# Dividing a pair of heads' outputs instead of the softmax weights, with casts and lo parts given to other engines

## The chip, the cores and the metric

The kernel runs on one core of a Trainium2 chip. A core has five engines with a queue each, and every engine works through its own queue in order: TensorE (PE in the profile; its weight loads are PEld), VectorE (DVE), ScalarE (ACT), GpSimd (POOL) and SyncE (SP), which here issues DMAs. The metric is the device time of one execution in microseconds (us), lower is better.

## What is computed

A two-layer encoder on 512 tokens of width 1024. Each layer normalises its input, projects it, runs four kinds of attention with four heads of 64 columns each, projects their concatenation back, and then runs a gated feed-forward block. Cut to what matters here:

```python
def one_block(args):                                   # b: differential attention
    s = einsum('bqhcd,bkhcd->bchqk', q_blk, k) * scale + bias
    p = jax.nn.softmax(s, axis=-1)
    a = p[:, 0] - lam * p[:, 1]
    return einsum('bhqk,bkhd->bqhd', a, v)             # then rms_norm(o, subln_g) * (1 - lam_init)
...
    out = jnp.sum(jnp.stack(outs) * wts, axis=0)       # c: dilated, three patterns merged by their sums
...
    p = jax.nn.softmax(s * scale, axis=-1)             # d: latent attention
    return einsum('bhqk,bkhd->bqhd', p, v)
...
mix = jnp.concatenate([o_a, o_b, o_c, o_d], axis=-1)   # o_a: 2D neighborhood attention
x = x + mix @ w_o[l]
h = rms_norm(x, ffn_norm[l])
x = x + (silu(h @ w_gate[l]) * (h @ w_up[l])) @ w_down[l]
```

All of it is in float32.

## The kernel before

Activations lie transposed: 128 features on the partitions, 512 tokens along the free dimension, eight such tiles for the width. TensorE multiplies in a rounded float32 format (fp32r in the profile), so each operand is split into a hi part, a cast of the value to that format, and a lo part, the value minus hi. A product is then three matmuls, hi by hi (L173), hi by lo (L175) and lo by hi (L178). The helper `split` does this for activations, with `copy` (L137 on ScalarE, L139 on VectorE or GpSimd) and `minus` (L142); `slab` does it for a slab of 1024 weight columns that came by DMA: a cast (L137 or L139) and a lo part (L160), which GpSimd makes in two halves of 512 columns and VectorE in one. `whi` and `wlo` have two buffers each. Which engine makes what stands in the table ENG by a tag ('P' GpSimd, 'V' VectorE, 'A' ScalarE); a tag that isn't in it goes to the default of its helper: ScalarE for casts, VectorE for the lo parts of activations, GpSimd for those of attention's weights. A tag holds for both layers.

An attention stage handles the four kinds in the order b, c, d, a (numbers 1, 2, 3, 0 in the code). For b, c and d a unit is one head and one block of 128 queries against all 512 keys; sixteen units each, by pair of heads p, head hh of the pair and block qb. For a there are eight larger units. A unit has three steps. S_ makes the scores in PSUM, `soft` (L676 to L688) adds the bias and takes the row's extreme `mx` on VectorE (L684; for d a plain reduction, L681), exponentiates on ScalarE with the row's sum `den` as a second output (L686) and takes its reciprocal `rd` on VectorE (L687), and `normalise` (L690 to L696) multiplies the 128x512 weights `e` by `rd`, on ScalarE (L692), GpSimd (L694) or VectorE (L696). For b, `s_b` does this with two score tiles: GpSimd multiplies the second by its `rd` and the negated lambda (L755), and VectorE adds the first times its own `rd` (L756). T_ transposes `e` on TensorE, four times 128x128 (L826), and splits the result into `th` (from PSUM, a cast) and `tl` (PSUM minus `th`, always VectorE). V_ multiplies with the values, and after a head's last block `fold` (L759 to L772) adds the two halves of PSUM; after the pair's second head `plain_fin` (c, d) splits the pair's output into a `mix` tile. `b_fin` first takes the root mean square of the rows: squares, column sums on TensorE, a power on GpSimd, and `spread_rows`, which copies the 128x8 result over 128x512 and transposes it so that it lies along the tokens (`obw`).

A loop of steps sets the order (`step`): S_ of the unit three ahead (LEAD), filler work (projections of later stages, output projections), V_ of the unit before, T_ of this one, filler again. The amounts of filler are written out by hand (RATES). The framework then schedules with a simulated time line and puts in all waits; buffers are recycled by tag: tag `ob` has one buffer, the small 128x1 tiles eight.

The feed-forward stage (from L1062) is a plain stream of matmuls over slabs of weights and isn't touched.

Of the kernel before, what the change touches and what calls it, by code (L numbers as in the profile page):

```python
# [42 lines left out]
RAW = 4  # L43
PRE = 0
NQF = 6
ENG = {'m10_l': 'P', 'wh_cq0': 'P', 'rk2': 'V', 'wh_ud1': 'V', 'ea03': 'A', 'wl_kc1': 'V', 'b11_l': 'P', 'fo100': 'V', 'kh_c01': 'V', 'kl_c00': 'P', 'ea13': 'A', 'sc_qn1': 'P', 'kl_d00': 'P', 'fa010': 'P', 'wl_wo04': 'V', 'wh_qb1': 'V', 'ql_d10': 'P', 'kd_d11': 'P', 'm11_h': 'V', 'kd_d01': 'P', 'ed03': 'A', 'wh_kb0': 'V', 'ql_a01': 'P', 'x22': 'P', 'wl_qa1': 'V', 'wh_qb0': 'V', 'ed11': 'P', 'kh_d11': 'V', 'wl_ka0': 'V', 'kl_a10': 'P', 'x27': 'P', 'ec11': 'A', 'wh_vcb': 'V', 'x05': 'P', 'ed13': 'A', 'sc_ka0': 'P', 't301_h': 'V', 'x03': 'P', 'fo010': 'V', 'wh_wo14': 'P', 'kd_d10': 'P', 'wl_wo16': 'V', 'wl_wo14': 'V', 'fa110': 'P', 'fo211': 'V', 'sc_ka1': 'P', 'x15': 'P', 'kl_a11': 'P', 'kd_a01': 'V', 'wh_wo00': 'P', 'wh_ckv': 'V', 'ed02': 'P', 'm30_l': 'P', 'wh_ur': 'V', 'wl_kb1': 'V', 'kh_a10': 'V', 'kl_d10': 'P', 'kd_a11': 'P', 'kh_a11': 'V', 'kd_d00': 'P', 'fo200': 'V', 'ed00': 'P', 'x23': 'P', 'm21_l': 'P', 'kh_d10': 'P', 'ea10': 'A', 'kl_a00': 'P', 'qh_a01': 'P', 'b10_l': 'P', 'fa300': 'P', 'm20_h': 'P', 'kh_c00': 'V', 't203_h': 'V', 'fo310': 'V', 'wl_wo12': 'V', 'x02': 'P', 't210_h': 'V', 'kd_a00': 'P', 'kl_c01': 'P', 'wl_qb1': 'V', 'ec13': 'A', 'rq1': 'V', 'wl_vbb': 'V', 't011_h': 'V', 't100_h': 'V', 'ea00': 'V', 't212_h': 'V', 'qh_c00': 'V', 'kh_c11': 'P', 'kh_d00': 'V', 'fa210': 'P'}
QS = 'ss'
WARM = 12
NV = 2
# [13 lines left out]
def tile_encoder(ctx, tc, xT, gains, lamv, w_in, w_kr, w_d, w_o0, w_o1, w_o2, w_gu, w_dn,  # L63
# [268 lines left out]
    def attention(l, xsrc, x, hs, ssq, pl, nar):  # L332
# [440 lines left out]

        def plain_fin(m):
            def fin(p, hh, pv):
                of = fold(m, p, hh, pv)
                if hh:
                    mt = mix_tile(m, p)
                    split(mt[:, 0, :], mt[:, 1, :], of, f"m{m}{p}")
                    ready.add((m, p))  # L780
            return fin

        def b_fin(p, hh, pv):
            of = fold(1, p, hh, pv)
# [6 lines left out]
            def sums():  # L791
# [73 lines left out]
        def grid_unit(p, hh, b2, need):  # L865
# [4 lines left out]
            def S_():  # L870
# [3 lines left out]
                for bb in range(2):  # L874
# [417 lines left out]
```

## Time and profile before

| | us |
|---|---|
| median of 3 runs (lowest to highest) | 1323.04 (1323.0 to 1323.88) |
| profiled execution | 1322.35 |
| its span, first to last instruction | 1320.5 |
| TensorE busy in the span | 1277.9 |
| VectorE busy | 770.0 |
| ScalarE busy | 563.5 |
| GpSimd busy | 457.2 |

The first attention stage takes about the first 298 us, the first feed-forward stage lasts to about 660, the second attention stage to about 945, and the second feed-forward stage to the end. Busy times over the whole span mix these stages; TensorE's busy time holds the modelled end of each matmul. The profile's words for engines are those of the first section; L142 is line 142 of the kernel; "idle before" is the time in which an engine did nothing ahead of an instruction, and the name behind it is what ended that.

### The profile page before, as it was taken

How to read it: one execution, taken by the hardware profiler on the slowest of the kernel's cores; microseconds unless marked ns; L12 is line 12 of the kernel's file. 1: busy time of each engine (PE TensorE's matmuls, PEld its weight loads, DVE VectorE, ACT ScalarE, POOL GpSimd, SP SyncE). 2: the span in 40 equal slices, each digit the busy share in tenths (PEclk: the TensorE clock that was granted, in tenths of full speed). 3: DMA queues.
4: the chain of work that ended last, by engine and by line, in shares of the span. 5: the costliest groups of instructions: out<-in, count | busy, mean ns of one | idle time of the engine just before them, and what ended most of it. 6: DMA issues, size and time to landing. Idle time of an engine off the chain costs nothing. (4 is left out here: it accounts for less than half of the span.)

```text
span 1320.5 us, 17193 instructions
## 1 busy us (share of the span) xinstructions
PE 1277.9 (97%) x6330; PEld 1066.6 (81%) x6330; DVE 770.0 (58%) x1315; ACT 563.5 (43%) x972; POOL 457.2 (35%) x377
## 2 busy tenths in 40 slices
PE   8999999989999999999999989999899999999997
PEld 7777788867888888888898777788688888888886
DVE  6589989866444444333237989887754444443232
ACT  5456666744333333222225666666533333332230
POOL 1267765544111111100145577454621111111000
PEclk9999999999999999999999999999999999999999
DMA  5652432122222223333345424321132222223321
GB/s 189 183 154 75 138 105 81 50 79 80 96 96 97 98 100 97 99 113 111 111 137 161 121 77 129 98 81 65 64 100 100 101 99 96 96 92 90 99 88 64
DMA packets 50916, 135.63 MB, mean 103 GB/s; under 512 B 7896, under 2 KB 12760, under 8 KB 50832
## 3 DMA queue, kind: packets, MB, share of 16 engines
q1 hardware_dynamic: 50544, 134.25, 32.3%
q8 instruction: 50, 0.82, 0.3%
q10 hardware_dynamic: 288, 0.29, 0.1%
q14 instruction: 34, 0.28, 0.1%
HBM read 119.01 MB, written 4.23 MB: 93 GB/s over the span
## 5 line engine op out<-in xcount | busy, mean ns | idle before, releaser
L175 PE MATMUL gu<-h_f,whi_gu 128*128 128x512 f32 x704 | 274.3, 390 | 1.5 <-DVE h_f L201 1.4
L173 PE MATMUL gu<-h_f,whi_gu 128*128 128x512 f32 x704 | 273.9, 390 | 0.1
L1081 POOL TENSOR_TENSOR u<-u,th 128x512 f32<-128x512 f32 x44 | 93.2, 2118 | 367.6 <-DVE u L1079 351.5
L178 PE MATMUL gu<-h_f,wlo_gu 128*128 128x512 f32 x704 | 173.9, 389 | 0.0
L175 PEld LDWEIGHTS gu<-h_f,whi_gu 128*128 128x128 f32 x704 | 132.0, 188 | 31.0 <-DVE h_f L201 4.0
L173 PEld LDWEIGHTS gu<-h_f,whi_gu 128*128 128x128 f32 x704 | 132.2, 188 | 28.2 <-DVE x L663 0.9
L178 PEld LDWEIGHTS gu<-h_f,wlo_gu 128*128 128x128 f32 x704 | 132.2, 188 | 27.4
L137 ACT CAST whi_gu<-raw_gu 128x1024 fp32r<-128x1024 f32 x88 | 92.7, 1054 | 105.3 <-PE gu L175 104.9
L173 PE MATMUL dn<-act,whi_dn 128*128 128x512 f32 x330 | 128.4, 389 | 0.0
L175 PE MATMUL dn<-act,whi_dn 128*128 128x512 f32 x330 | 128.4, 389 | 0.0
L160 DVE TENSOR_TENSOR wlo_gu<-raw_gu,whi_gu 128x1024 fp32r<-128x1024 f32 x88 | 111.3, 1264 | 19.4 <-ACT whi_gu L137 17.8
L686 ACT ACTIVATE e<-e,mx 128x512 f32<-128x512 f32 (+1 forms) x128 | 85.5, 669 | 73.0 <-DVE mx L684 70.9
L160 DVE TENSOR_TENSOR wlo_dn<-raw_dn,whi_dn 128x1024 fp32r<-128x1024 f32 (+1 forms) x45 | 51.0, 1134 | 100.3 <-PE dn L178 60.9
L1079 DVE SCALAR_TENSOR_TENSOR u<-gu,bc_ff 128x512 f32<-128x512 f32 x44 | 30.4, 691 | 122.8 <-PE gu L178 122.8
L137 ACT CAST whi_dn<-raw_dn 128x1024 fp32r<-128x1024 f32 (+1 forms) x45 | 44.2, 982 | 127.8 <-PE dn L175 111.3
L137 ACT CAST act<-u 128x512 fp32r<-128x512 f32 x44 | 27.3, 621 | 155.1 <-POOL u L1081 155.1
L178 PE MATMUL dn<-act,wlo_dn 128*128 128x512 f32 x330 | 82.1, 389 | 0.0
L142 DVE TENSOR_TENSOR tl<-tp,th 128x512 fp32r<-128x512 f32 x112 | 74.5, 683 | 10.3 <-ACT th L137 9.6
L684 DVE CUSTOM_DVE_ANT_0 e<-sc,t 128x512 f32<-128x512 f32 x96 | 65.1, 684 | 21.3 <-PE sc L751 8.8
L142 DVE TENSOR_TENSOR act<-u,act 128x512 fp32r<-128x512 f32 x44 | 32.7, 743 | 73.6 <-ACT act L137 73.3
L178 PEld LDWEIGHTS dn<-act,wlo_dn 128*128 128x128 f32 x330 | 62.0, 188 | 12.8
L173 PEld LDWEIGHTS dn<-act,whi_dn 128*128 128x128 f32 x330 | 62.0, 188 | 12.8
(433 smaller groups left out, 2719.4 us busy)
## 6 DMA issues: line engine op xcount, KB each, us to landing
raw_gu<-in_w_gu_dram SPq DMA_DIRECT2D x88, 512.0 KB, 3.2
raw_dn<-in_w_dn_dram SPq DMA_DIRECT2D x32, 512.0 KB, 3.5
raw_wo<-in_w_o_dram SPq DMA_DIRECT2D x16, 512.0 KB, 3.9
t<-tb SPq DMA_DIRECT2D x16, 448.0 KB, 3.9
raw_dn<-in_w_dn_dram SPq DMA_DIRECT2D x16, 384.0 KB, 3.1
sb<-kbn SPq DMA_DIRECT2D x64, 64.0 KB, 2.0
sb<-qbn SPq DMA_DIRECT2D x64, 64.0 KB, 2.1
xin<-in_xT_dram SPq DMA_DIRECT2D x8, 256.0 KB, 5.2
```

Of the source, the lines that this page charges most:

```text
L137: nc.scalar.copy(out, src)
L142: engine(tag, usual).tensor_tensor(out, src, hi.bitcast(F32), op=ALU.subtract)
L160: lo_eng.tensor_tensor(lo[:, c], raw[:, c], hi[:, c].bitcast(F32), op=ALU.subtract)
L173: nc.tensor.matmul(pt, whi[:, k, wcol], xs[k][:, 0, :], start=first and k == 0, stop=False)
L175: nc.tensor.matmul(pt, whi[:, k, wcol], xs[k][:, 1, :], start=False, stop=False)
L178: nc.tensor.matmul(pt, wlo[:, k, wcol], xs[k][:, 0, :], start=False, stop=last and k == nk - 1)
L684: nc.vector.tensor_tensor_reduce(out=e, in0=sc, in1=bias, scale=1.0, scalar=BIG, op0=ALU.add, op1=ALU.min, accum_out=mx)
L686: nc.scalar.activation(e, src, AF.Exp, bias=mx, scale=-1.0, accum_out=den)
L1079: nc.vector.scalar_tensor_tensor(u, pts[1], 0.5, r_bc, op0=ALU.mult, op1=ALU.mult)
L1081: nc.gpsimd.tensor_tensor(u, u, th, op=ALU.mult)
```

## The change

In c and d the weights `e` stay unnormalised. `soft` writes each row's sum into a column of a 128x8 tile of the pair (`sums`); when the last unit of a pair has its exp, `row_factors` takes one reciprocal of the eight columns and lets ScalarE spread it over a 128x512 tile `rep` of tag `ob`; `plain_fin` transposes `rep` on TensorE and multiplies the folded output by it. In b the second weights tile is multiplied by the one factor w = den0 * rd1 * (-lambda) inside VectorE's combining instruction, the step on GpSimd goes, and the sum of the first is brought in where the rows' root mean square is taken (`norms`). Heads a keep their division, with its reciprocal now in `grid_unit`.

In ENG, 23 casts go to ScalarE: from VectorE `fo` (5 tags), `kh` (6), `qh_c00`, `m11_h` and `t..._h` (6), from GpSimd `kh_c11`, `kh_d10`, `m20_h`, `qh_a01`. 27 lo parts go from VectorE to GpSimd: `kl` (5), `ql` (10), `m11_l`, `m20_l`, `m31_l`, and nine of weights (`wl_ka0`, `wl_kb1`, `wl_kc1`, `wl_qa1`, `wl_vbb`, `wl_wo04`, `wl_wo12`, `wl_wo14`, `wl_wo16`). `rk2`, `rq1`, `kd_a01` and some whole-weight casts stay on VectorE. RATES, LEAD and the order of the work stay.

```diff
-            return nar.tile([P, 1], F32, tag=tag, name=f"{tag}_{nm}", bufs=8)
-
-        def soft(e, sc, bias, nm):
-
-            mx, den, rd = small("mx", nm), small("den", nm), small("rd", nm)
+            return nar.tile([P, 1], F32, tag=tag, name=f"{tag}_{nm}", bufs=6)
+
+        def sums(m, p):
+
+            if ("den", m, p) not in g:
+                g["den", m, p] = nar.tile([P, 8], F32, tag="den8", name=f"den{m}{p}_{l}", bufs=3)
+            return g["den", m, p]
+
+        def soft(e, sc, bias, nm, den):
+
+            mx = small("mx", nm)
...
             nc.scalar.activation(e, src, AF.Exp, bias=mx, scale=-1.0, accum_out=den)
-            nc.vector.reciprocal(rd, den)
-            return rd
+
+        def row_factors(m, p):
+
+            rc = nar.tile([P, 8], F32, tag="den8r", name=f"rc{m}{p}_{l}", bufs=2)
+            nc.vector.reciprocal(rc, sums(m, p))
+            t = g["rep", m, p] = pl.tile([P, 4, 2, 64], F32, tag="ob", name=f"rep{m}{p}_{l}", bufs=1)
+            nc.scalar.copy(t, rc.rearrange("p (h c) -> p c h", h=2).unsqueeze(3).to_broadcast([P, 4, 2, 64]))
...
             e = e_tile(nm)
-            rd = soft(e, sc, None, nm)
-            normalise(e, rd, f"ed{p}{qb}")
+            c = 4 * hh + qb
+            soft(e, sc, None, nm, sums(3, p)[:, c : c + 1])
             return e
...
-            (e0, e1), (r0, r1) = es, rs
-            nc.gpsimd.tensor_scalar(e1, e1, r1, nlam[l], op0=ALU.mult, op1=ALU.mult)
-            nc.vector.scalar_tensor_tensor(e0, e0, r0, e1, op0=ALU.mult, op1=ALU.add)
-            return e0
+                soft(es[c], sc, t5_bias(2 * p + hh, qb), f"{nm}{c}", ds[c])
+            rd, w = small("rd", nm), small("rd", f"{nm}w")
+            nc.vector.reciprocal(rd, ds[1])
+            nc.vector.tensor_scalar(w, ds[0], rd, nlam[l], op0=ALU.mult, op1=ALU.mult)
+            nc.vector.scalar_tensor_tensor(es[0], es[1], w, es[0], op0=ALU.mult, op1=ALU.add)
+            return es[0]
...
             def fin(p, hh, pv):
+                if hh:
+                    rows = stat_bank(f"rows{m}{p}{l}")
+                    t = g["rep", m, p]
+                    for c in range(4):
+                        nc.tensor.transpose(rows[:, c * P : (c + 1) * P], t[:, c].rearrange("p h d -> p (h d)"), ident)
                 of = fold(m, p, hh, pv)
                 if hh:
                     mt = mix_tile(m, p)
+                    nc.vector.tensor_tensor(of, of, rows, op=ALU.mult)
                     split(mt[:, 0, :], mt[:, 1, :], of, f"m{m}{p}")
...
-                nc.vector.tensor_scalar(col, pt[:, :8], 1.0 / 64, EPS, op0=ALU.mult, op1=ALU.add)
+                r0 = nar.tile([P, 8], F32, tag="den8r", name=f"obd{p}_{l}", bufs=2)
+                nc.vector.reciprocal(r0, sums(1, p))
+                nc.vector.scalar_tensor_tensor(col, pt[:, :8], 1.0 / 64, r0, op0=ALU.mult, op1=ALU.mult)
+                nc.vector.tensor_tensor(col, col, r0, op=ALU.mult)
+                nc.vector.tensor_scalar(col, col, EPS, None, op0=ALU.add)
                 rc = nar.tile([P, 8], F32, tag="bcol", name=f"obr{p}_{l}", bufs=2)
                 nc.gpsimd.tensor_tensor(rc, col, mhalf, op=ALU.pow)
+                nc.vector.tensor_tensor(rc, rc, r0, op=ALU.mult)
...
                 u["e"] = score(p, hh, qb, nm)
+                if m > 1 and hh and qb == 3:
+                    row_factors(m, p)
```

## Rows read from the trace of the kernel before

**Rows 1.** Windows: us, busy (instructions) of PE, PEld, DVE, ACT, POOL; clock; DMA.
```profile
363.00:396.00 33.00, 33.00 (x147) 27.32 (x146) 15.19 (x19) 10.08 (x12) 6.41 (x3) 1.00 0.29 96
...
55.00:130.00 75.00, 70.06 (x355) 57.05 (x354) 66.14 (x143) 46.26 (x96) 51.00 (x45) 0.98 0.45 138
130.00:185.00 55.00, 51.96 (x284) 43.69 (x283) 49.53 (x101) 34.57 (x69) 38.83 (x41) 0.94 0.41 120
...
695.00:795.00 100.00, 93.10 (x515) 78.23 (x513) 85.76 (x189) 62.10 (x131) 60.71 (x57) 0.98 0.41 121
...
sum 458.00, PE 436.68 PEld 368.11 DVE 391.74 ACT 289.27 POOL 278.22; mean PE 54.58 PEld 46.01 DVE 48.97 ACT 36.16 POOL 34.78
```

**Rows 2.** Lines of TensorE: out<-in, count, busy us, mean ns, idle before.
```profile
L173 PE MATMUL gu<-h_f,whi_gu 128*128 128x512 f32 x704 | 273.9, 390 | 0.1
```

**Rows 3.** TensorE's waits, 55 to 280, then 695 to 928: us, times, longest.
```profile
PE sc L383 <- DVE mx L684: 2.7, 2, 2.2
...
PE uk L173 <- DVE v_d L395: 0.2, 1, 0.2
...
PE tp L826 <- DVE e L756: 2.8, 2, 2.2
...
PE pv L838 <- DVE rd L687: 0.2, 1, 0.2
```

**Rows 4.** Timeline of VectorE at 155 and at 766 us: start, duration.
```profile
154.97 4.54 DVE L139 CAST ks_d<-kn 64x512 fp32r<-64x512 f32 x1
...
766.06 2.98 DVE L534 TENSOR_TENSOR krb<-krf,ropek 32x512 f32<-32x512 f32 x1
```

**Rows 5.** Lines of VectorE, whole run.
```profile
L139 DVE CAST th<-tp 128x512 fp32r<-128x512 f32 x24 | 16.4, 684 | 1.1 <-PE pv L838 0.9
...
L139 DVE CAST mix<-o 128x512 fp32r<-128x512 f32 x2 | 0.8, 421 | 0.0
...
L142 DVE TENSOR_TENSOR qs_a<-qa,qs_a 64x512 fp32r<-64x512 f32 x6 | 7.4, 1235 | 0.2
...
L142 DVE TENSOR_TENSOR ks_a<-ka,ks_a 64x512 fp32r<-64x512 f32 x2 | 1.4, 690 | 0.1
...
L160 DVE TENSOR_TENSOR wlo_wo<-raw_wo,whi_wo 128x1024 fp32r<-128x1024 f32 x8 | 11.1, 1387 | 0.1
...
L160 DVE TENSOR_TENSOR wlo_vbb<-raw_vbb,whi_vbb 128x1024 fp32r<-128x1024 f32 x1 | 1.2, 1219 | 0.0
...
L696 DVE TENSOR_SCALAR e<-e,rd 128x512 f32<-128x512 f32 x12 | 7.6, 634 | 0.6
...
L687 DVE RECIPROCAL rd<-den 128x1 f32<-128x1 f32 x160 | 23.8, 155 | 11.4 <-ACT e L686 10.4
...
L756 DVE SCALAR_TENSOR_TENSOR e<-e,rd,e 128x512 f32<-128x512 f32 x32 | 31.8, 997 | 0.9 <-POOL e L755 0.8
```

**Rows 6.** Lines of ScalarE, whole run.
```profile
L137 ACT CAST th<-tp 128x512 fp32r<-128x512 f32 x88 | 50.0, 584 | 25.3 <-PE tp L826 13.0 <-PE pv L838 8.7 <-PE tp L895 2.8
...
L692 ACT ACTIVATE e<-e,rd 128x512 f32<-128x512 f32 x16 | 11.6, 724 | 17.4 <-DVE rd L687 17.4
```

**Rows 7.** Lines of GpSimd, whole run.
```profile
L694 POOL TENSOR_SCALAR e<-e,rd 128x512 f32<-128x512 f32 x36 | 28.4, 789 | 27.5 <-DVE rd L687 23.5 <-PE tp L826 3.2 <-DVE col_kv L250 0.6
L755 POOL TENSOR_SCALAR e<-e,rd,nlam 128x512 f32<-128x512 f32 x32 | 26.4, 824 | 55.3 <-DVE rd L687 50.5 <-PE kr L526 2.6 <-DVE obc L796 1.9
...
L160 POOL TENSOR_TENSOR wlo_wo<-raw_wo,whi_wo 128x512 fp32r<-128x512 f32 x16 | 22.0, 1395 | 29.4 <-ACT whi_wo L137 21.1 <-PE ip_ka L178 4.1 <-ACT e L686 4.1
```

**Rows 8.** Timeline of TensorE: a group of four transposes and what follows it.
```profile
110.24 0.60 PE L826 MATMUL tp<-ident,e 128*128 128x128 f32 x4
110.60 0.47 PE L523 MATMUL kr<-h_a,whi_kr 128*128 128x512 f32 x1
```

**Rows 9.** Windows in two stretches, all engines.
```profile
150.00:180.00 30.00, 27.25 (x130) 22.25 (x130) 28.31 (x48) 16.38 (x30) 23.35 (x22) 0.89 0.34 99
795.00:825.00 30.00, 27.00 (x150) 22.59 (x150) 28.62 (x54) 19.25 (x38) 24.59 (x25) 1.00 0.46 126
```

More of the change, by code (lines that the diff above doesn't have):

```diff
@@ L45 @@
 NQF = 6
-ENG = {'m10_l': 'P', 'wh_cq0': 'P', 'rk2': 'V', 'wh_ud1': 'V', 'ea03': 'A', 'wl_kc1': 'V', 'b11_l': 'P', 'fo100': 'V', 'kh_c01': 'V', 'kl_c00': 'P', 'ea13': 'A', 'sc_qn1': 'P', 'kl_d00': 'P', 'fa010': 'P', 'wl_wo04': 'V', 'wh_qb1': 'V', 'ql_d10': 'P', 'kd_d11': 'P', 'm11_h': 'V', 'kd_d01': 'P', 'ed03': 'A', 'wh_kb0': 'V', 'ql_a01': 'P', 'x22': 'P', 'wl_qa1': 'V', 'wh_qb0': 'V', 'ed11': 'P', 'kh_d11': 'V', 'wl_ka0': 'V', 'kl_a10': 'P', 'x27': 'P', 'ec11': 'A', 'wh_vcb': 'V', 'x05': 'P', 'ed13': 'A', 'sc_ka0': 'P', 't301_h': 'V', 'x03': 'P', 'fo010': 'V', 'wh_wo14': 'P', 'kd_d10': 'P', 'wl_wo16': 'V', 'wl_wo14': 'V', 'fa110': 'P', 'fo211': 'V', 'sc_ka1': 'P', 'x15': 'P', 'kl_a11': 'P', 'kd_a01': 'V', 'wh_wo00': 'P', 'wh_ckv': 'V', 'ed02': 'P', 'm30_l': 'P', 'wh_ur': 'V', 'wl_kb1': 'V', 'kh_a10': 'V', 'kl_d10': 'P', 'kd_a11': 'P', 'kh_a11': 'V', 'kd_d00': 'P', 'fo200': 'V', 'ed00': 'P', 'x23': 'P', 'm21_l': 'P', 'kh_d10': 'P', 'ea10': 'A', 'kl_a00': 'P', 'qh_a01': 'P', 'b10_l': 'P', 'fa300': 'P', 'm20_h': 'P', 'kh_c00': 'V', 't203_h': 'V', 'fo310': 'V', 'wl_wo12': 'V', 'x02': 'P', 't210_h': 'V', 'kd_a00': 'P', 'kl_c01': 'P', 'wl_qb1': 'V', 'ec13': 'A', 'rq1': 'V', 'wl_vbb': 'V', 't011_h': 'V', 't100_h': 'V', 'ea00': 'V', 't212_h': 'V', 'qh_c00': 'V', 'kh_c11': 'P', 'kh_d00': 'V', 'fa210': 'P'}
@@ new lines @@
+ENG = {'b10_l': 'P', 'b11_l': 'P', 'ea00': 'V', 'ea03': 'A', 'ea10': 'A', 'ea13': 'A', 'ec11': 'A', 'ec13': 'A', 'ed00': 'P', 'ed02': 'P', 'ed03': 'A', 'ed11': 'P', 'ed13': 'A', 'fa010': 'P', 'fa110': 'P', 'fa210': 'P', 'fa300': 'P', 'kd_a00': 'P', 'kd_a01': 'V', 'kd_a11': 'P', 'kd_d00': 'P', 'kd_d01': 'P', 'kd_d10': 'P', 'kd_d11': 'P', 'kl_a00': 'P', 'kl_a01': 'P', 'kl_a10': 'P', 'kl_a11': 'P', 'kl_c00': 'P', 'kl_c01': 'P', 'kl_c10': 'P', 'kl_c11': 'P', 'kl_d00': 'P', 'kl_d01': 'P', 'kl_d10': 'P', 'kl_d11': 'P', 'm10_l': 'P', 'm11_l': 'P', 'm20_l': 'P', 'm21_l': 'P', 'm30_l': 'P', 'm31_l': 'P', 'ql_a00': 'P', 'ql_a01': 'P', 'ql_a10': 'P', 'ql_a11': 'P', 'ql_c00': 'P', 'ql_c01': 'P', 'ql_c10': 'P', 'ql_c11': 'P', 'ql_d00': 'P', 'ql_d01': 'P', 'ql_d10': 'P', 'ql_d11': 'P', 'rk2': 'V', 'rq1': 'V', 'sc_ka0': 'P', 'sc_ka1': 'P', 'sc_qn1': 'P', 'wh_ckv': 'V', 'wh_cq0': 'P', 'wh_kb0': 'V', 'wh_qb0': 'V', 'wh_qb1': 'V', 'wh_ud1': 'V', 'wh_ur': 'V', 'wh_vcb': 'V', 'wh_wo00': 'P', 'wh_wo14': 'P', 'wl_qb1': 'V', 'x02': 'P', 'x03': 'P', 'x05': 'P', 'x15': 'P', 'x22': 'P', 'x23': 'P', 'x27': 'P'}
@@ L728, in s_c @@
             e = e_tile(nm)
-            rd = soft(e, sc, t5_bias(4 + 2 * p + hh, qb), nm)
-            normalise(e, rd, f"ec{p}{qb}", "P")
+            c = 4 * hh + qb
+            soft(e, sc, t5_bias(4 + 2 * p + hh, qb), nm, sums(2, p)[:, c : c + 1])
             return e
@@ L746, in s_b @@
             t = slice(qb * P, (qb + 1) * P)
-            es, rs = [], []
+            i = 4 * hh + qb
+            es, ds = [], [sums(1, p)[:, i : i + 1], small("den", nm)]
             for c in range(2):
@@ L752, in s_b @@
                 es.append(e_tile(f"{nm}{c}"))
-                rs.append(soft(es[c], sc, t5_bias(2 * p + hh, qb), f"{nm}{c}"))
-            (e0, e1), (r0, r1) = es, rs
-            nc.gpsimd.tensor_scalar(e1, e1, r1, nlam[l], op0=ALU.mult, op1=ALU.mult)
-            nc.vector.scalar_tensor_tensor(e0, e0, r0, e1, op0=ALU.mult, op1=ALU.add)
-            return e0
+                soft(es[c], sc, t5_bias(2 * p + hh, qb), f"{nm}{c}", ds[c])
[4 more added lines that the diff above has]
+            return es[0]
         def fold(m, p, hh, pv):
@@ L789, in b_fin, with norms @@
             nc.scalar.activation(sq, of, AF.Square)
-            def sums():
+            def norms():
                 pt = stat_bank(f"obm{p}{l}")
@@ L806, in rows @@
                 ready.add((1, p))
-            after(AFT[0], sums)
+            after(AFT[0], norms)
             after(AFT[1], rows)
@@ L880, in S_ @@
                     bt = g["ab"][0 if b < 3 else 1][:, 2 * p + hh].rearrange("p s k -> p (s k)")
-                    rd = soft(e[:, c], sc[:, c], bt, f"{nm}{bb}")
+                    den, rd = small("den", f"{nm}{bb}"), small("rd", f"{nm}{bb}")
+                    soft(e[:, c], sc[:, c], bt, f"{nm}{bb}", den)
+                    nc.vector.reciprocal(rd, den)
                     normalise(e[:, c], rd, f"ea{p}{b}", "P")
```

## The prediction

> **What bounds the kernel now.** I read the windows first: busy time of each engine by stretch, with TensorE's granted clock. In the feed-forward part TensorE never pauses: 147 matmuls in 33 us, 224.5 ns from one to the next [rows 1], though each is shown as 390 ns long [rows 2]; the rest, 0.165 us, is its modelled end, which overlaps the next. The change touches nothing there. In the middle of the two attention stages (55 to 280 and 695 to 928 us, 458 us in all) the picture is another: TensorE is busy 436.7 us, but VectorE 391.7, which is 86% of the whole and 86 to 90% in the three stretches shown, against 63% for ScalarE and 61% for GpSimd [rows 1]. So TensorE has the most work, VectorE is nearly full, and both run their queues in order. The question is how much TensorE loses to VectorE.
>
> Then the waits of TensorE in these two stretches: 8 rows with 9.0 us in 12 waits, and 10 rows with 11.7 us in 14 waits; nearly all name VectorE (`mx`, `e`, `rd`, `tl`, `va`) [rows 3]. A wait is counted only from the modelled end, so each hides 0.165 us: 26 x 0.165 = 4.3 us. After long waits the granted clock stands at the lower of its two levels (1.2 of 2.4 GHz) for a while, and the mean of the stretch falls: 0.94 over 55 us is 3.3 us lost, 0.98 over 75 is 1.5, 0.98 over 100 is 2.0, 6.8 together [rows 1]. Price of all the waits on VectorE: 20.7 + 4.3 + 6.8 = **31.8 us**. That is what relief of VectorE can give at most. TensorE's waits outside these stretches (start, first weights, the last output tiles, the ends of the feed-forward) hang on things that the change leaves as they are.
>
> The timeline shows what such a wait looks like. At 154.97 us VectorE begins the cast of a key tile, `ks_d<-kn`, 64x512, and holds its queue for 4.54 us, where the 24 casts of `th`, with twice the partitions, take 0.684 each [rows 4, 5]; the wait of 2.2 us for `mx` in the first stretch is for the score tile behind it [rows 3]. So it is not VectorE's sum alone: `ks_d<-kn` has all its operands in SBUF and `th<-tp` reads PSUM, and it is the former kind that can be stretched, as `qs_a<-qa,qs_a` at a mean of 1235 ns against 690 of the like `ks_a<-ka,ks_a` [rows 5].
>
> **The change on VectorE.** Off it, over both layers [rows 5]: casts and copies to ScalarE, seven groups from `th` (24, 16.4 us) down to `mix` (2, 0.8 us), 39.3 us; lo parts of q, k and mix to GpSimd, seven groups from `qs_a` (7.4) to `ks_a` (1.4), 34.4 us; lo parts of weights to GpSimd, six groups from `wlo_wo` (11.1) to `wlo_vbb` (1.2), 22.3 us; the normalising multiply L696 of 512 columns, 7.6 us; of the 160 reciprocals L687 the 64 of heads c and d, 64 x 0.155 = 9.9 us (in b, one of two reciprocals becomes a 128x1 multiply, taken at the same 0.155). Sum 113.5. Onto it: eight multiplies by `rows` in plain_fin, 128x512 from SBUF and PSUM, at the 684 ns of `th`, which reads PSUM too: 5.5 us; eight reciprocals of 128x8 and four small instructions more in each of four `norms`, 24 x 0.155 = 3.7. Net 104 us less: 391.7 becomes about 288, 63% of the stretches.
>
> **On ScalarE.** 50 casts from VectorE and 8 from GpSimd, at the 584 ns of `th` there [rows 6]: 33.9 us; eight copies that spread a 128x8 column over 128x512, for which I take 0.6 as for a cast (the trace has none on ScalarE; between the 0.584 of `th` and the 0.724 of L692): 4.8; minus the 16 normalising multiplies L692, 11.6 us [rows 6]. Net +27, 289.3 becomes 316, 69%.
>
> **On GpSimd.** Off: L694 of 512 columns 28.4, L755 26.4, eight casts at the 0.79 of L694, 6.3: 61.1 [rows 7]. On: 30 lo parts of q and k and 6 of mix, and 17 slabs of weights in two halves, all at the 1.395 of half a `wlo_wo` [rows 7]: 70 x 1.395 = 98 us. Net +37: 278.2 becomes 315, 69%. Three engines then stand at 63 to 69%, and none near full on the average.
>
> **On TensorE.** Eight groups of four transposes. A group that is there now starts at 110.24 and the next matmul at 110.60, so 0.36 us each [rows 8]: **+2.9 us**, and none of it is covered, since TensorE is the fullest engine. The transposes need `rep`, which ScalarE writes after VectorE's reciprocal, which waits for the exp of the pair's last unit. On ScalarE the following exps and casts are queued behind that copy, on VectorE the next units' `mx`. `rep` also shares the single buffer of tag `ob` with `obw`: the first one of pair (2,0) is made three units ahead and can't be written before `rows` of pair (1,1) has read. The trace doesn't have this wait. From below: nothing, since a pair's factors are ready about four units before its end (three of lead, and one more to V_). From above: the longest wait on VectorE, 2.2 us, at all eight places: 17.6 [rows 3]. The multiply by `rows` also stands ahead of the last mix tile, whose lo part m31 goes from 0.69 to 1.40 us [rows 5, 7]. I take **+3.0** for all new waits, near the lower end, by those four units.
>
> In the units of b the GpSimd step (0.82 us) between exp and the combining multiply L756 goes, and two 128x1 steps on VectorE stay. So the chain is shorter by some 0.7 us, but VectorE's load there hardly falls, and what holds it there stays on it: `krb`, 32x512 and all in SBUF, took 2.98 us at 766 us, ahead of waiting score tiles, and `rk2` keeps it on VectorE [rows 4]; L756, with two SBUF tensors, has a mean of 997 ns [rows 5].
>
> **How much of the 31.8 goes.** The waits behind things that move (the key casts, the q lo parts, the normalising in c and d) lie mostly after 130 and 795 us; those behind `krb` and L756 lie before. I take 56% as gone, 17.9 us, between a quarter (8.0) and all. Sum: -17.9 + 2.9 + 3.0 = **-12.0**. The profiled execution took 1322.35 us, its span 1320.5 and 1.85 around it; less 12.0 that is 1310.4. The median of the runs, 1323.04, lies 0.7 above it, so I forecast **1311.0**.
>
> The row of the 4.54 us cast [rows 4] bears on a rule. The Trainium skill, page "SBUF — State Buffer", section "Who interferes with whom", says that a VectorE instruction with two SBUF inputs or in a two-port mode contends with GpSimd, and that whichever issues second is blocked until the first ends. By that rule 37 us more of GpSimd work would hold what stays on VectorE (`krb`, L756, `cn_q`) longer than now, and relief would be at the lower end, as in the second rival.
>
> **The rivals.**
> First, all waits on VectorE vanish, since at 63% nothing queues: -31.8 + 2.9 = -28.9, so 1294. For it: 104 of 392 us leave. Against it: b keeps its load, and `krb` its place. Chance 0.13.
>
> Second, relief is given back: GpSimd's added work holds L756 and `krb`, or ScalarE's exps stand behind casts, and only a quarter goes: -8.0 + 2.9 + 3.0 = -2.1, so 1321. For it: L756 at 997 ns shows such holding already [rows 5]. Against: L755's 26.4 us of GpSimd leave the very stretches in which L756 runs. Chance 0.14.
>
> Third, on the other side, GpSimd becomes the bound where the q and k of d and the first output weights are made. From 150 to 180 us it is busy 23.35 us, from 795 to 825 24.59 [rows 9]. Off these: four and five L694 and one cast at 0.79, 4.0 and 4.7. On: five lo parts of q and k of d, one of mix, and two slabs (`wo`, `ka`), ten instructions at 1.395, 14.0 [rows 7]. That makes 33.4 and 33.9 us in 30. If TensorE has to wait for the excess, it is 3.4 + 3.9 = 7.3, and two more stretches at the lower clock at 1.7 each (half of the 3.3 above); the waits of VectorE that would have gone come back as waits on lo parts (relief near zero): 7.3 + 3.4 + 2.9 = +13.6; less some 7 of relief that b's waits still give (a fifth of 31.8), +7, so 1330. It decides when GpSimd's work in a stretch exceeds the stretch by more than three units of lead and the second buffer of `wlo` can absorb. For it: the sum is over 30. Against: it is so in 60 of 458 us, and its mean over all is 69%. Chance 0.17. Beside it stands a rule of the Trainium skill, page "GPSIMD Engine Reference", its opening: GpSimd is the wrong choice for ordinary elementwise arithmetic, which VectorE does about twice as fast. The rows agree on the size (a slab: 2 x 1.395 us against 1.387 on VectorE) [rows 5, 7].
>
> That the change doesn't do what it says: the list of engines names every moved tile, so this could only be in the order that the scheduler gives the instructions; that is in the rivals' waits.
>
> **How the numbers follow.** Forecast 0.56, rivals 0.13, 0.14, 0.17. About 0.2% (2.6 us) is what a measurement of this kernel can tell from no change. The second rival lies within that; the forecast and the first are faster: faster 0.69, same 0.14, slower 0.17. The range of 8 in 10 reaches from the first rival's edge, 1295, to 1328, short of the third rival's centre; about 0.07 is left out below and 0.10 above. From a quarter of relief with new waits of 8 (1326) to nearly all with none it holds the bounds of the unknown costs; new waits of 17.6 with a quarter lie beyond it.
>
> **What would show it.** Right: VectorE near 63% in the attention stages, no `ks_d` cast there, TensorE's waits on VectorE near 9 us instead of 20.7, those after 130 and 795 us gone first, GpSimd near 69%. The transposes of `rows` would wait under 0.5 us each. Wrong: rows of TensorE waiting for `wlo`, `qs_d` or `ks_d` of GpSimd or for casts of ScalarE; more stretches below the full clock; L756 over 1.0 us.

## The result and the profile after

| | before | after |
|---|---|---|
| median (lowest to highest), us | 1323.02 (1320.56 to 1323.88) | 1307.03 (1305.89 to 1307.29) |
| profiled execution, us | 1322.35 | 1306.79 |
| its span, us | 1320.5 | 1305.0 |
| first attention stage, to its last matmul ahead of the feed-forward | 297.7 | 288.7 |
| second attention stage, from its first matmul (`v_b`) to that point | 285.5 | 278.8 |

The ratio is 0.9878, its 95% interval 0.9862 to 0.9894: 16.0 us less, against the 12.0 forecast. Both attention stages are shorter, by 9.0 and 6.7 us; the feed-forward is not. First the page's line of busy times, then the windows of [rows 1] in after (the columns are the same). The sum is that of the mid-parts of the two stages, 55 to 262 and 685 to 911 us, which answer to the 225 and 233 us of the longer stages in [rows 1] (the kernel before has the same 9.0 and 11.7 us of TensorE's waits in these narrower stretches):

```profile
PE 1275.5 (98%) x6362; PEld 1067.1 (82%) x6362; DVE 687.6 (53%) x1168; ACT 588.8 (45%) x1022; POOL 474.9 (36%) x371
```

```profile
363.00:396.00 33.00, 33.00 (x148) 27.31 (x147) 15.19 (x19) 10.08 (x12) 6.41 (x3) 1.00 0.27 96
55.00:130.00 75.00, 74.50 (x393) 61.92 (x393) 65.95 (x151) 53.36 (x114) 47.55 (x39) 1.00 0.48 147
130.00:185.00 55.00, 54.30 (x312) 45.55 (x311) 36.28 (x75) 41.80 (x84) 41.36 (x40) 1.00 0.43 124
...
sum 433.00, PE 424.58 PEld 360.46 DVE 309.48 ACT 309.43 POOL 286.17; mean PE 212.29 PEld 180.23 DVE 154.74 ACT 154.72 POOL 143.09
```

Against [rows 1], TensorE does 393 matmuls in the first stretch where it did 355, and 312 where it did 284, and the granted clock is 1.00 where it was 0.98 and 0.94. VectorE falls most after 130 us, from 49.5 to 36.3. All of TensorE's waits in these two mid-parts (columns as in [rows 3]):

```profile
PE pv L866 <- DVE tl L142: 1.0, 2, 0.5
PE sc L764 <- DVE mx L690: 0.5, 2, 0.3
PE ip_va L173 <- ACT whi_va L137: 0.3, 1, 0.3
PE sc L383 <- DVE mx L690: 0.2, 1, 0.2
...
PE sc L383 <- DVE mx L690: 1.6, 1, 1.6
PE sc L764 <- DVE mx L690: 1.4, 1, 1.4
PE tp L853 <- DVE e L770: 1.2, 2, 1.0
PE pv L866 <- DVE tl L142: 1.2, 3, 0.5
PE tp L853 <- DVE tl L142: 0.4, 1, 0.4
PE rows L794 <- ACT rep L699: 0.3, 1, 0.3
```

That is 2.0 us in 6 waits and 6.1 in 9, 8.1 in all, where [rows 3] had 9.0 and 11.7. No row names a lo part of GpSimd.

### The profile page after: what moved, and what is told of

Its sections match the earlier page's. It is cut to its first block, busy times and chain, and to the rows that moved or that the text cites. A ratio compares the mean times of both kernels' runs of the same rounds, so it can differ in the third digit from the quotient of the medians.

```text
span 1305.0 us, 17103 instructions
## 1 busy us (share of the span) xinstructions
PE 1275.5 (98%) x6362; PEld 1067.1 (82%) x6362; DVE 687.6 (53%) x1168; ACT 588.8 (45%) x1022; POOL 474.9 (36%) x371
## 5 line engine op out<-in xcount | busy, mean ns | idle before, releaser
L690 DVE CUSTOM_DVE_ANT_0 e<-sc,t 128x512 f32<-128x512 f32 x96 | 65.0, 684 | 32.3 <-PE tp L853 12.6
L175 PEld LDWEIGHTS dn<-act,whi_dn 128*128 128x128 f32 x330 | 61.9, 188 | 12.9
L173 PEld LDWEIGHTS dn<-act,whi_dn 128*128 128x128 f32 x330 | 61.9, 188 | 12.8
```

What stands on the lines that cost most here:

```text
L173: nc.tensor.matmul(pt, whi[:, k, wcol], xs[k][:, 0, :], start=first and k == 0, stop=False)
L175: nc.tensor.matmul(pt, whi[:, k, wcol], xs[k][:, 1, :], start=False, stop=False)
```

## The experiments

The forecast's theory was that VectorE's load decides: take work off it and TensorE's waits on it go. The rivals were that work on GpSimd holds what stays on VectorE, and that something else in the change makes the gain. After a first batch of single parts the question became which combination is needed. "The two stretches" below are 55 to 262 and 685 to 911 us of each kernel's own trace, 433 us; a slower kernel has less of its stages in them, so VectorE's time of the whole run stands beside theirs in the table at the end. The kernel before took 1322.8 beside the first four of these runs and 1322.7 beside the others. The framework writes each kernel's order from its own time line, so every variant also has its own order on TensorE from some matmul on; differences of 2 or 3 us between variants can't be put down to the edit alone.

**Division alone.** The new division in b, c and d, with the old table of engines:

```diff
-ENG = (table of after)
+ENG = (table of before)
```

> The new way to divide with the engine table of before. VectorE loses about 17 us (64 reciprocals, the normalising L696) and gets 9, GpSimd loses 55 us of multiplies by rd, TensorE gets 2.9 us of transposes. Theory A, the sum: VectorE's total decides, each us taken off it is worth about 0.18 us (18.9 us of relief for 104 us): -1.5 + 2.9, so 1324. Theory B, the holds: VectorE's SBUF instructions held by GpSimd cause the waits, so 55 us less on GpSimd make them shorter: -6 + 2.9, so 1320.

Measured: 1326.46, ratio 1.0026 [1.0017, 1.0035], slower than before; both theories missed. TensorE's longest wait was for `e` at 116 us. VectorE's timeline ahead of it (start, duration), then GpSimd's, then TensorE's:

```profile
108.02 0.69 DVE L139 CAST whi_ckv<-raw_ckv 128x1024 fp32r<-128x1024 f32 x1
...
109.60 0.15 DVE L818 SCALAR_TENSOR_TENSOR obc<-obm,obd 128x8 f32<-128x8 f32 x1
109.72 0.91 DVE L770 SCALAR_TENSOR_TENSOR e<-e,rd_11030w,e 128x512 f32<-128x512 f32 x1
110.55 1.24 DVE L819 TENSOR_TENSOR obc<-obc,obd 128x8 f32<-128x8 f32 x1
...
114.96 1.60 DVE L534 TENSOR_TENSOR krb<-krf,ropek 32x512 f32<-32x512 f32 x1
...
116.79 2.54 DVE L139 CAST whi_ur<-raw_ur 128x256 fp32r<-128x256 f32 x1
119.26 0.74 DVE L770 SCALAR_TENSOR_TENSOR e<-e,rd_11100w,e 128x512 f32<-128x512 f32 x1
```

```profile
116.71 1.25 POOL L535 TENSOR_TENSOR kra<-kra,krb 32x512 f32<-32x512 f32 x1 [0.69 <-DVE krb L534]
117.93 1.25 POOL L785 TENSOR_TENSOR o<-o,oh 64x512 f32<-64x512 f32 x1
```

```profile
120.14 1.09 PE L853 MATMUL tp<-ident,e 128*128 128x128 f32 x4 [4.13 <-DVE e L770]
```

The combining multiply was behind a small weight cast that stood for 2.54 us, until two GpSimd instructions in a row had ended. So here the chain without the step on GpSimd was held up in VectorE's queue instead. (The profiled execution, 1330.87 us, is the slowest of eleven and 4.4 above their median.)

**Engines alone.** The old division with the new table (`ENG` of after in the kernel before).

> The old way to divide with the new engine table. VectorE loses about 96 us, GpSimd gets 92 and stands near 81% in the middle of the attention stages. Theory A, the sum: 96 x 0.18 = -17, so 1306. Theory B, the holds: the instructions that were held have mostly left VectorE, but GpSimd's own multiplies by rd now queue behind lo parts; -8 to -12, so 1311 to 1315.

Measured: 1324.23, ratio 1.001 [0.9998, 1.0022]; both missed. VectorE had all its relief, and TensorE waited as before, 21.9 us in the two mid-parts. The windows' sum, and the first waits of each mid-part:

```profile
sum 433.00, PE 410.72 PEld 346.54 DVE 301.09 ACT 304.06 POOL 331.67; mean PE 205.36 PEld 173.27 DVE 150.54 ACT 152.03 POOL 165.84
```

```profile
PE sc L717 <- ACT e L686: 3.3, 1, 3.3
PE tp L826 <- DVE rd L687: 3.0, 1, 3.0
PE tp L826 <- DVE e L756: 1.8, 2, 1.2
...
PE tp L826 <- DVE e L756: 4.0, 3, 2.0
PE sc L717 <- ACT e L686: 3.7, 1, 3.7
```

Over the whole run VectorE is as busy as in after (688.2 and 687.6 us), yet TensorE's 410.7 is far below after's 424.6. This is the run that speaks plainest against the forecast's theory. Its waits have more than one kind. Scores of d wait 3.3 and 3.7 us for an exp of ScalarE; ahead of the first, ScalarE works from 191.87 us through `ka`, two copies of outputs, the weight cast `whi_qa` and a `th`, and the exp starts at 195.13. And VectorE's combining multiply in b now waits for GpSimd's step, 6.5 us in six places, where [rows 5] have 0.8:

```profile
L756 DVE SCALAR_TENSOR_TENSOR e<-e,rd,e 128x512 f32<-128x512 f32 x32 | 34.9, 1092 | 6.7 <-POOL e L755 6.5
```

**Half of the casts alone**, in the kernel before: the 11 tags whose cast reads PSUM or the folded outputs, then the 8 tags of keys, queries and m11 with all operands in SBUF; each left out of the table, which sends them to ScalarE.

```diff
-'fo010': 'V', 'fo100': 'V', 'fo200': 'V', 'fo211': 'V', 'fo310': 'V',
-'t011_h': 'V', 't100_h': 'V', 't203_h': 'V', 't210_h': 'V', 't212_h': 'V', 't301_h': 'V',
```

> The kernel before with only those casts and copies given to ScalarE that read PSUM: 24 of th and 10 of fo, 23.3 us of VectorE. Theory A, the sum: 23.3 x 0.18 = -4.2, so 1319. Theory B, the holds: these instructions are never held, so nothing or -1: 1322 to 1323.

```diff
-'kh_a10': 'V', 'kh_a11': 'V', 'kh_c00': 'V', 'kh_c01': 'V',
-'kh_d00': 'V', 'kh_d11': 'V', 'qh_c00': 'V', 'm11_h': 'V',
```

> The kernel before with only those casts given to ScalarE that read SBUF: kh, qh and m11_h, 26 instances... of which VectorE has 16.0 us. Theory A, the sum: 16.0 x 0.18 = -2.9, so 1320. Theory B, the holds: the cast of 4.54 us at 155 us and the two stretches at the lower clock behind it go, with some of the second attention stage: -5 to -8, so 1315 to 1318.

Measured: 1323.74 and 1323.78, both 1.0009 [1.0, 1.0017]. Theory A missed twice; the first run is near the "nothing" of theory B, the second missed theory B too: the cast of 4.54 us [rows 4] was gone, and the waits came back as `rd` 1.9 and 3.0 us and `e` 1.2 and 2.4. One held instruction taken away is not a wait taken away.

**Lo parts back on VectorE**, in the changed kernel (27 tags):

```diff
-'ql_d00': 'P', 'kl_d01': 'P', 'm31_l': 'P',
+'ql_d00': 'V', 'kl_d01': 'V', 'm31_l': 'V', 'wl_ka0': 'V',
...
```

> The changed kernel with the 27 lo parts back on VectorE (57 us there, some 92 us off GpSimd). Theory C, the pairing: the new division takes GpSimd out of the chain from exp to the transposes and so makes room for lo parts; both are needed, so most of the 16 us is lost: 1317 to 1322. Theory D, the order: each queue's order is planned for times that don't come true, and any other table shifts where a queue's head waits; the loss is then not tied to the kind of work and may be anything from 3 to 18 us.

Measured: 1307.10, ratio 0.9886 [0.9872, 0.9899], the time of after with VectorE at 352.0 us of the stretches instead of 309.5 and GpSimd at 214.3 instead of 286.2. Theory C falls: with the casts moved, moving the lo parts too neither gains nor costs.

**Casts back** where they were (19 tags to VectorE, four to GpSimd):

```diff
+'kh_d00': 'V', 't011_h': 'V', 'fo010': 'V', 'm11_h': 'V',
...
+'kh_c11': 'P', 'kh_d10': 'P', 'm20_h': 'P', 'qh_a01': 'P',
```

> The changed kernel with the casts where they were (39 us back on VectorE, 6 on GpSimd, 35 off ScalarE). Theory C, the pairing: casts are not what needed room on GpSimd; VectorE rises by 39 us and gets back its held key casts, so a part is lost: 1311 to 1315. Theory D, the order: anything from 3 to 18 us lost.

Measured: 1315.05, ratio 0.9943 [0.993, 0.9955], 8.0 us above after, the upper end of theory C's range and inside theory D's. From the division alone (1326.5) this kernel differs in the lo parts only: with the casts where they were, moving the lo parts gains 11.4 us.

**Heads b divided as before**, in the changed kernel:

```diff
-nc.vector.scalar_tensor_tensor(es[0], es[1], w, es[0], op0=ALU.mult, op1=ALU.add)
+nc.gpsimd.tensor_scalar(e1, e1, r1, nlam[l], op0=ALU.mult, op1=ALU.mult)
+nc.vector.scalar_tensor_tensor(e0, e0, r0, e1, op0=ALU.mult, op1=ALU.add)
```

> The changed kernel with heads b divided as before (GpSimd's 26 us between exp and the combining multiply come back, the small instructions of norms go). Theory C, the pairing: GpSimd stands in b's chain again behind lo parts, in b alone: 1311 to 1315. Theory D, the order: anything from 0 to 18 us lost.

Measured: 1317.0, ratio 0.9953 [0.9939, 0.9967], 10.0 us above after, although VectorE fell to 297.9 (678.9 over the whole run); above theory C's range, inside theory D's. TensorE's longest wait, 3.0 us, is at 104 to 107 us. GpSimd's timeline shows the multiply of b, L769 there, behind two lo parts; below it VectorE's, then TensorE's:

```profile
101.34 2.55 POOL L160 TENSOR_TENSOR wlo_qc<-raw_qc,whi_qc 128x512 fp32r<-128x512 f32 x2
103.87 1.21 POOL L769 TENSOR_SCALAR e<-e,rd,nlam 128x512 f32<-128x512 f32 x1
```

```profile
103.02 0.16 DVE L766 RECIPROCAL rd<-den 128x1 f32<-128x1 f32 x1
103.29 1.15 DVE L485 SCALAR_TENSOR_TENSOR cn_q<-cq,gn,cn_q 128x512 fp32r<-128x512 f32 x1
104.36 0.68 DVE L142 TENSOR_TENSOR tl<-tp,th 128x512 fp32r<-128x512 f32 x1
105.07 0.69 DVE L781 TENSOR_TENSOR o<-o,pv 64x512 f32<-64x512 f32 x1
105.80 0.75 DVE L770 SCALAR_TENSOR_TENSOR e<-e,rd,e 128x512 f32<-128x512 f32 x1
```

```profile
106.69 1.09 PE L848 MATMUL tp<-ident,e 128*128 128x128 f32 x4 [3.04 <-DVE rd L766]
```

GpSimd's multiply ended at 105.08, after 0.7 us behind the lo parts, but it isn't what ended last: VectorE was busy with three other instructions until 105.76, and the combining multiply (L770) came right behind them. So this wait shows the place that the combining multiply got in VectorE's order; that the step on GpSimd is why it got so late a place is not shown. (The engines alone have the same wait of 3.0 us behind the same three instructions.) Where GpSimd did end last shows in VectorE's idle time ahead of L770, 7.0 us in seven places, the longest 2.5 us behind two lo parts at 736 us; there TensorE had other work and didn't wait.

```profile
L770 DVE SCALAR_TENSOR_TENSOR e<-e,rd,e 128x512 f32<-128x512 f32 x32 | 35.2, 1101 | 7.1 <-POOL e L769 7.0
```

Nearly all of the loss is in the first layer: its attention stage takes 298.5 us, 9.8 more than in after, the second 280.1, 1.3 more, with the same edit in both. Behind the wait of 3.0 us the granted clock of 106 to 112 us is 0.56.

**No sums at the outputs of c and d.** The changed kernel without `row_factors`, the 32 transposes and the multiply by `rows`, so that c and d stay undivided:

```diff
-nc.tensor.transpose(rows[:, c * P : (c + 1) * P], t[:, c].rearrange("p h d -> p (h d)"), ident)
...
-nc.vector.tensor_tensor(of, of, rows, op=ALU.mult)
...
-row_factors(m, p)
```

> The changed kernel without bringing the sums of c and d into the outputs: no spread copy, no transposes of rep, no multiply by rows (so c and d stay undivided). Its difference from the changed kernel is the price of that step: the prediction has 2.9 for the transposes and 3.0 for waits, so 1301; with the transposes alone 1304; under theory D, the order, it may even be slower than the changed kernel.

Measured: 1305.08, ratio 0.9862 [0.9849, 0.9876]. By the medians the whole step costs 2.0 us, where the forecast had 2.9 + 3.0; the interval overlaps that of after, so its price is small and not known better.

**c and d divided as before**, the rest as changed:

```diff
-soft(e, sc, t5_bias(4 + 2 * p + hh, qb), nm, sums(2, p)[:, c : c + 1])
+soft(e, sc, t5_bias(4 + 2 * p + hh, qb), nm, den)
+nc.vector.reciprocal(rd, den)
+normalise(e, rd, f"ec{p}{qb}", "P")
```

> The changed kernel with the division of heads c and d put back (sums brought out on VectorE, reciprocal, transpose of the reciprocals and the multiply on GpSimd in the chain of the folded heads); heads a and b, the casts and the lo parts stay as changed. Theory 'GpSimd out of the chain': what the division gains, it gains where GpSimd stood between a score and a later matmul; c's and d's stage on GpSimd comes back into such a chain, so most of the gain goes, as it did with b's division put back (1317.0): 1312 to 1318 us. Theory 'b alone': b's hop has the shortest time to the matmul that wants it, and c's and d's has work between: 1305 to 1309 us, and the step at the outputs (2.0 us by the run without it) would even be given back.

Measured: 1315.81, ratio 0.9947 [0.9933, 0.9961], 8.8 us above after: the first theory's time, and not that of b alone. (The normalising multiply comes back on GpSimd, ScalarE and VectorE, by the table, not on GpSimd alone.) VectorE stood at 313.4. The longest wait, TensorE's line and then GpSimd's queue ahead of it:

```profile
176.18 1.97 PE L849 MATMUL tp<-ident,e 128*128 128x128 f32 x8 [4.72 <-POOL e L705]
```

```profile
168.75 2.65 POOL L142 TENSOR_TENSOR qs_d<-qn,qs_d 64x512 fp32r<-64x512 f32 x2
171.44 0.60 POOL L139 CAST ks_d<-ks_d 64x512 fp32r<-64x512 f32 x1
172.11 1.25 POOL L142 TENSOR_TENSOR ks_d<-kn,ks_d 64x512 fp32r<-64x512 f32 x1
173.41 0.61 POOL L139 CAST ks_d<-ks_d 64x512 fp32r<-64x512 f32 x1
174.07 1.26 POOL L142 TENSOR_TENSOR ks_d<-kn,ks_d 64x512 fp32r<-64x512 f32 x1
175.43 0.69 POOL L705 TENSOR_SCALAR e<-e,rd 128x512 f32<-128x512 f32 x1
```

VectorE had written the last reciprocals by 170.6 us; the multiply, 0.69 us long, began at 175.43 because it stood behind parts of keys and queries in GpSimd's queue, and VectorE had nothing else to do. Here GpSimd's queue did end last. Behind the wait the granted clock falls (columns as in [rows 1]):

```profile
176.00:185.00 9.00, 8.82 (x36) 7.58 (x37) 4.77 (x12) 3.82 (x8) 8.72 (x10) 0.69 0.23 59
```

That is 2.8 us lost, and with the 4.7 us of the wait 7.5. The first attention stage takes 297.4 us, 8.7 more than in after; the second, with the same edit, takes 277.2, 1.6 less. So nearly the whole price of this edit is one wait in one layer and the clock behind it.

**Half of the casts back on VectorE**, in the changed kernel: first the 11 tags of the first half above, then the 8 of the second.

> The changed kernel with those moved casts put back on VectorE whose input lies in PSUM or that head the value products (the two families of the exponentials' transposes and of the folded outputs, 11 tags); the SBUF casts of keys and queries stay on ScalarE. Theory 'SBUF hold': an SBUF-only cast on VectorE can be held for microseconds beside GpSimd, a PSUM one cannot, so this loses 0 to 1 us: 1307 to 1308. Theory 'chain': the cast of the transposed exponentials lies in the chain from scores to values and shares VectorE with the next head's subtraction, so this loses most of the 8 us that all casts are worth (1315.05 with all of them back): 1312 to 1315.

> The changed kernel with only the SBUF casts of keys, queries and their second factors put back on VectorE (8 tags); the casts of the exponentials' transposes and of the folded outputs stay on ScalarE. Theory 'SBUF hold': one cast of 64x512 took 4.54 us on VectorE in the kernel before, and such holds make most of the 8 us: 1313 to 1315. Theory 'chain': these casts run ahead of what wants them, 0 to 2 us lost: 1307 to 1309. If this run and the one with the other half put back both lose under 3 us, the 8 us belong to neither half alone and the casts act only together.

Measured: 1303.86, ratio 0.9867 [0.985, 0.9884], by the medians faster than after by 3.2 us, which neither theory had (the two intervals overlap, and by the ratios it is 1.5, so it is a small gain at best); and 1308.49, ratio 0.9895 [0.9881, 0.991], 1.5 us above after (2.2 by the ratios, and again the intervals overlap), as the chain theory had it. All casts back cost 8.0; these halves cost next to nothing. But they are not the whole: the run with all casts back also returned four cast tags to GpSimd (`kh_c11`, `kh_d10`, `m20_h`, `qh_a01`), which are in neither half. So the 8 us may come from the halves together or from these four; no run separates them.

**More off VectorE.** The casts of whole weights and one key factor to ScalarE, two steps on d's keys and queries (`rk2`, 32x512, and `rq1`, 128x512) and the norms' 128x8 steps to GpSimd:

```diff
-'wh_ckv': 'V', 'wh_kb0': 'V', 'wh_qb0': 'V', 'wh_qb1': 'V', 'wh_ud1': 'V', 'wh_ur': 'V', 'wh_vcb': 'V', 'kd_a01': 'V',
-'rk2': 'V', 'rq1': 'V',
+'rk2': 'P', 'rq1': 'P',
...
-nc.vector.tensor_tensor(rc, rc, r0, op=ALU.mult)
+nc.gpsimd.tensor_tensor(rc, rc, r0, op=ALU.mult)
```

> The changed kernel with what still reads only SBUF on VectorE taken off it: the casts of the whole weights go to ScalarE, the copy of the keys' first factor too, two small row factors and the three 128x8 steps of the norms go to GpSimd. Theory 'SBUF hold': the norms' 128x8 steps on VectorE took 558 to 874 ns each beside GpSimd, and the casts go with the holds, 2 to 5 us faster than the changed kernel: 1302 to 1305. Theory 'saturated': TensorE waits for only 8.1 us in the middle stretches of the changed kernel and none of the waits names these steps, so nothing moves: 1306 to 1308. Theory 'new hop': the norms on GpSimd put its handover back on the way to the outputs, slower: 1309 to 1315.

Measured: 1310.95, ratio 0.991 [0.9897, 0.9923], 3.9 us above after with the lowest VectorE of all, 295.7; the third theory's time, but not its mechanism, since no wait names the norms. The first wait of its mid-parts names a power of GpSimd that the edit didn't touch. Its input was written by 137.91 us, and it began at 140.38, behind two steps on the queries, one of them (L556) the `rq1` that the edit had moved there:

```profile
PE rows_kv L266 <- POOL rcol_kv L252: 1.6, 1, 1.6
```

The larger part of the loss is in the second attention stage, 282.0 us against 278.8, and there the longest wait, 2.0 us, is for a copy of ScalarE (`oh`) and the granted clock of 685 to 911 us is 0.98 against 1.00.

All runs in order of time, with the two attention stages of the profiled execution, VectorE's busy time in the two stretches and in the whole run, and GpSimd's in the stretches:

| kernel | us | first stage | second stage | VectorE | VectorE, whole run | GpSimd |
|---|---|---|---|---|---|---|
| changed, first half of the casts back | 1303.9 | 290.2 | 273.9 | 330.6 | 710.5 | 292.2 |
| changed, sums not brought out | 1305.1 | 288.9 | 276.7 | 305.3 | 681.5 | 287.6 |
| changed | 1307.0 | 288.7 | 278.8 | 309.5 | 687.6 | 286.2 |
| changed, lo parts back | 1307.1 | 286.5 | 280.3 | 352.0 | 730.2 | 214.3 |
| changed, second half of the casts back | 1308.5 | 288.5 | 283.3 | 318.6 | 701.1 | 285.1 |
| changed, more off VectorE | 1311.0 | 289.9 | 282.0 | 295.7 | 675.1 | 292.4 |
| changed, all casts back | 1315.1 | 291.0 | 284.9 | 336.8 | 722.1 | 293.7 |
| changed, c and d divided as before | 1315.8 | 297.4 | 277.2 | 313.4 | 696.7 | 309.8 |
| changed, b divided as before | 1317.0 | 298.5 | 280.1 | 297.9 | 678.9 | 310.8 |
| before | 1322.7 | 297.7 | 285.5 | 375.9 | 770.0 | 271.1 |
| before, first half of the casts moved | 1323.7 | 300.1 | 286.8 | 359.5 | 755.0 | 271.4 |
| before, second half of the casts moved | 1323.8 | 299.8 | 285.9 | 369.3 | 763.5 | 273.9 |
| before, new engines | 1324.2 | 300.2 | 285.2 | 301.1 | 688.2 | 331.7 |
| before, new division | 1326.5 | 307.0 | 284.7 | 358.5 | 763.2 | 215.0 |

## Why the prediction was right, and where not

**The time** lies in the range, in the direction of the forecast and 4.0 us below it. But the runs give the gain another owner than the sum did, so that the number came out near is in part luck.

**The step that failed** is "How much of the 31.8 goes". It tied the waits on VectorE to the VectorE work that moves; by that the new table alone was expected at about 1306 (theory A), and it took 1324.2. The paragraph ahead of that step saw that in b the GpSimd step goes and the chain is shorter, but priced that at nothing because VectorE's load there hardly falls. The runs show that it counts: with the engines as changed, b's division put back costs 10.0 us and c's and d's 8.8, while VectorE's time in those runs is lower than after's or nearly the same (678.9 and 696.7 us against 687.6). How it counts is less clear. In c and d one wait of 4.7 us, with GpSimd's queue ahead of the multiply, and the lower clock behind it are nearly the whole price; in b the longest wait stands behind VectorE's own queue. And both prices fall in the first layer: in the second the same edits cost 1.3 us and gain 1.6. So they are what one place in one order lost, not a price for each unit, and theory D, the order, explains them as well; a run with the old division that holds TensorE's order fixed would tell, and was not made.

**Neither part alone gains, together they do.** The new division with VectorE's queue nearly as full as it was (763.2 of 770.0 us) gave +3.7 us; the new engines with the chain as it was gave +1.4, within the noise of none; both gave -16. With the new division the table's two parts can be told apart:

| new division, us | lo parts as before | lo parts to GpSimd |
|---|---|---|
| casts as before | 1326.5 | 1315.1 |
| casts to ScalarE | 1307.1 | 1307.0 |

So with the short chain relief of VectorE does count, up to a point: the casts alone give the whole gain, the lo parts alone 11.4 us of it, and with the casts moved they add nothing. With the old division neither half of the casts gained; all casts, or the lo parts, without the new division were not run. Total VectorE time doesn't order the runs: 730.2 us stood in one of 1307, 722.1 in one of 1315. That the order each kernel got decides the rest is likely, but not shown.

**The amount of relief.** 56% of 31.8 was taken, 17.9. The waits fell from 20.7 to 8.1 (forecast "near 9"), 12.6; 11 waits fewer hide 11 x 0.165 = 1.8; the clock stands at 1.00 in the stretches of [rows 1], 6.8 (each mean is rounded to 0.01, so this is good to about 1 us). That is 21.2, or 67%, an under-sized term by 3.3. The new waits, taken at 3.0, are one row of 0.3 us; transposes and all, the step costs about 2.0, not 5.9 (the run without it, whose interval overlaps that of after). These two terms would make -21.2 + 2.0 = -19.2; the stages show -15.7, so some 3.5 us more were lost at places that this sum doesn't hold. Some 1.9 of them can be read at the end of the first stage: the granted clock is 0.87 from 262 to 289 us, 3.5 us lost, where the kernel before has 0.91 from 280 to 298, 1.6 lost.

**VectorE's total.** 104 us off was forecast; the page has 770.0 before and 687.6 after, 82.4. The multiply by `rows` was right (684 forecast), the small steps were not: 155 ns was taken for each, and the 32 factors w of b (L769) took 260 to 276, the three steps of the norms that have all operands in SBUF 558 to 874 in the mean, and the copy `rep_ob`, which the change doesn't touch, is at 1439 where it had 681 before. Lines of after (mean ns is the second number behind the bar):

```profile
L819 DVE TENSOR_TENSOR obc<-obc,obd 128x8 f32<-128x8 f32 x4 | 3.0, 759 | 0.0
L820 DVE TENSOR_SCALAR obc<-obc 128x8 f32<-128x8 f32 x4 | 2.2, 558 | 0.0
L823 DVE TENSOR_TENSOR obr<-obr,obd 128x8 f32<-128x8 f32 x4 | 3.5, 874 | 0.0
L263 DVE COPY rep_ob<-obr 128x512 f32<-128x512 f32 x4 | 5.8, 1439 | 0.0
L798 DVE TENSOR_TENSOR o<-o,rows 128x512 f32<-128x512 f32 x8 | 5.4, 677 | 0.0
```

Summed by durations as the forecast summed them, VectorE lost 94 us of instructions. The other 12 were never there to gain: neighbours overlap, as at 109.72 in the trace of the division alone, where L770 is shown 0.91 us long and L819 starts 0.83 after it, and busy time counts the overlap once.

**GpSimd** did not become the bound, the third rival. Its lo parts were forecast at 1.395 us each; they took a little less. The first line below is of the weights, the second of queries, and the third is ScalarE's copy `rep`, forecast at 0.6 us:

```profile
L160 POOL TENSOR_TENSOR wlo_wo<-raw_wo,whi_wo 128x512 fp32r<-128x512 f32 x32 | 41.3, 1312 | 21.9 <-ACT whi_wo L137 11.0 <-PE tp L924 5.8 <-ACT rep L699 4.8
L142 POOL TENSOR_TENSOR qs_d<-qn,qs_d 64x512 fp32r<-64x512 f32 x8 | 10.7, 1335 | 1.0 <-ACT qs_d L137 0.4
L699 ACT COPY rep<-rc 128x512 f32<-128x512 f32 x8 | 4.9, 616 | 3.6 <-DVE rc L697 2.9 <-DVE o L828 0.7
```

In the two stretches GpSimd stands at 66%, ScalarE at 71, VectorE at 71 (forecast 69, 69, 63). The rival was right in one thing: GpSimd's queue does cost TensorE, where something on the chain is in it, as in the run with c and d divided as before; the change took that out of b, c and d.

**The rule on contention** would have put relief at the lower end; relief came out at 67%. The holds it speaks of are there, the next section has their numbers, but in after TensorE's waits that name `e` (L770), one of the instructions the rule would hold, are 1.2 us, and L770's mean is 967 ns, where "over 1.0 us" was a sign of being wrong. Putting 42.5 us of lo parts (352.0 less 309.5) back on VectorE, and taking 72 off GpSimd, changed the time by 0.1 us; that run changes load and contention at once, so it doesn't show that each is worth nothing.

## What to carry to other kernels

Price a move between engines by the chain it shortens or lengthens as well as by the load it takes off: ask what stands in the queue of each engine that a result passes on its way to the bounding engine. Before forecasting that a full engine's waits go with its work, look whether another step lies in the same chain, since then neither edit alone may show a gain. When a variant costs some microseconds, look in each layer before calling it the price of the edit: here the same edit cost 9 us in one layer and next to nothing in the other. Busy times of single engines, three of them below 75%, say little about any of this.

## What the hardware showed that was not expected

A VectorE instruction with all operands in SBUF can stand for longer than one GpSimd instruction takes: the 128x256 cast `whi_ur` of the division alone was shown 2.54 us long and ended as two GpSimd instructions of 1.25 us, one right behind the other, had ended. The same cast has a mean of 0.28 us in the kernel before, and one four times as wide took 0.69 us at 108.02, where GpSimd sat idle until 108.79. The cast of 4.54 us [rows 4] is alike: it ended at 159.51, and four GpSimd instructions stood end to end from 154.29 to 159.23. The Trainium skill, page "SBUF — State Buffer", section "Who interferes with whom", says that in a two-port mode the engine that issues second is blocked for the whole of the other's instruction; here the stand spans two and four of them, so a run of GpSimd instructions is the size to reckon with (which mode these casts ran in, no row here shows). And size is no protection: a 128x8 multiply of two SBUF tensors took 1.24 us at 110.55, beside GpSimd's lo parts, where the 128x8 step at 109.60, which reads PSUM, took 0.15.
